# Two sets of level tiles and a keys-first order for the delta heads in an encoder layer kernel

## The chip, the cores and the metric

The kernel runs on one core of one Trainium2 chip. The metric is the device time of one execution in microseconds (us); the time before is the median of three runs, 1550.36 us (1548.67 to 1551.51).

## What is computed

One layer of a bidirectional encoder over 1024 tokens of width 1024: a mixer, a cross-attention into 256 memory tokens, and a SwiGLU layer, each with a norm before and after. Only the mixer is touched. It projects the normed input once; some columns feed a windowed attention with rotary positions, others a gated DeltaNet that runs over the sequence in both directions.

```python
h = _rms_norm(x, g_mix_pre[l])
proj = h @ w_in[l]
aq, ak, av, dqkv, dgate, dalpha, dbeta = jnp.split(proj, IN_SPLITS, axis=-1)
aq = _rope(aq.reshape(b, s, ATTN_HEADS, ATTN_HEAD_DIM), positions)
...
attn_o = _window_attention(aq, ak, av, attn_sink[l])
dn_o = _gated_deltanet(dqkv, dgate, dalpha, dbeta, ...)
mix = jnp.concatenate([attn_o, dn_o], axis=-1) @ w_out[l]
```

Within a chunk the DeltaNet solves a unit lower triangular system. For head, direction and chunk, `k` the normed keys:

```python
decay = jnp.exp(jnp.where(incl, g[..., :, None] - g[..., None, :], -jnp.inf))
kb = k * beta[..., None]
lower = jnp.where(strict, jnp.einsum('bhnid,bhnjd->bhnij', kb, k) * decay, 0.0)
tmat = lower + jnp.eye(c, dtype=jnp.float32)
sol = lax.linalg.triangular_solve(tmat, rhs, left_side=True, lower=True, unit_diagonal=True)
```

The kernel uses chunks of 128 tokens (8 of them), which gives the same result. There are 4 delta heads and 2 directions.

## The kernel before

**Stages.** The normed input is turned into `hT` (high and low parts of each 512-token half). A projection of 128 columns (`proj`, `gemm_b`, L261) is 48 matrix products into two `pg` banks, of which there are three; the weights are loaded (`load_w`) and split into `whi` and `wlo`. Then come, in this order:

1. *Delta stage* (to about 227 us): for each of the heads 0 to 3, keys, queries and values are projected (`delta_proj`), convolved over 5 taps on ScalarE and VectorE (`conv`), and prepared (`prep`). `prep` makes the decay matrix `E`, turns keys, values and queries with TensorE (`turned`), takes lengths, forms `U` (keys by keys, times `E`, stored to `d_u`), the scaled keys and values in one tile `kv` (stored to `d_kv`), and the masked query products `pm` (stored to `d_pz`). `base_inverse(g)` follows for each pair of heads: it reads the 32x32 diagonal blocks of `U` back into a tile `V`, builds `A`, and solves all 32x32 triangles at once with 60 small VectorE operations (L534, L536), then stores the results to `d_inv`. Each of its tiles has one buffer. `ORDER_1` is the order of these steps; `save` holds the last `pm` stores back until the second inverse's loads are issued.
2. *Levels and projections* (227 to about 360 us). `levels(h)` joins the 32x32 inverses to 64 and then to 128: 20 small loads (`fetch`, L551) put the blocks on the diagonals of the wide tiles `D5`, `D6`, `Z0`, `Z1` (128 x 8 x 128) and into `m5`, two loads bring `Ul`, and then TensorE, ScalarE and VectorE take turns: transposes of `Ul` (L576) give `L5` and `L6`, a product and its copy `bs` and a second product (L585, L591) give `z5`, which is put into `D6` and `Z`, and the same once more with `L6`, `mov6` gives the outer blocks of `Z`, which are stored. There is one set of the wide tiles, so each head's fetches wait for the head before. `ORDER_2` mixes the levels with the attention projections `A0` to `A4` (`A4` makes the keys), the values `V`, the gates `G0` to `G3` and pairs of windows `W`. `attn_proj` multiplies a projected half by sine and cosine (`sn`, `rop`), sends `sn` through four transfers that rotate its partitions into `rot2`, adds, splits into `qhi` and `qlo`, and stores both. `value_proj` copies a half to `vT` and transposes it (`ptv`, L749).
3. *Windows, scan, memory keys* (to about 594 us), under `ORDER_3`. A window loads its queries `qs`, takes scores `psw` against the keys `khi`, `klo`, does a softmax on VectorE and ScalarE, transposes (`ptw`) and multiplies with the values (`pow`). The scan (`psc`) reads `d_kv` and `d_pz`.
4. The rest of the layer, which starts with the mixer's output projection (L1016).

**What sets the order.** The three `ORDER` lists say in which order the steps are written. A scheduler then fixes each engine's own order when the program is built; on the chip each engine runs its list strictly in order. All transfers are issued by SyncE's queue, one after the other; a transfer that waits holds all that stand behind it. A tile's tag and `bufs` give the number of buffers that its users share: the next user of a buffer waits until the last one has been read.

Of the kernel before, what the change touches and what calls it, by code (L numbers as in the profile page):

```python
# [19 lines left out]
P = 128  # L20
# [55 lines left out]
def tile_hybrid_block(  # L76
# [121 lines left out]
    def small():  # L198
        return ps.tile([P, 512], F32, tag="ps", name="ps")
# [76 lines left out]
    def conv(pp, ci):  # L276
        cp = tcv.tile([P, S + 4], F32, tag="cp", name="cp", bufs=2)
        nc.gpsimd.memset(cp[:, 0:2], 0.0)
        nc.gpsimd.memset(cp[:, S + 2:S + 4], 0.0)
        acc = tcv.tile([P, S], F32, tag="acc", name="acc", bufs=3)  # L280
        taps = [cols[:, t * 12 + ci:t * 12 + ci + 1] for t in range(5)]
        for hf in range(2):
            nc.scalar.copy(cp[:, 2 + hf * HALF:2 + (hf + 1) * HALF], pp[hf])
            nc.scalar.activation(acc[:, hf * HALF:(hf + 1) * HALF], pp[hf], AF.Identity, scale=taps[2])  # L284
        for t in (0, 1, 3, 4):
            nc.vector.scalar_tensor_tensor(acc, cp[:, t:t + S], taps[t], acc, ALU.mult, ALU.add)  # L286
        nc.scalar.activation(acc, acc, AF.Silu)
        return acc
# [125 lines left out]

    unsaved = []

    def save(after=None):

        while unsaved:
            with ExitStack() as order_:  # L420
                if after:
                    order_.enter_context(tc.issue_after(after.ins))
                nc.sync.dma_start(*unsaved.pop(0))

    def prep(h, kc, qc, vc):

        g, hh = h // 2, h % 2
        for src, slot in ((kc, 2), (qc, 3)):
            nc.sync.dma_start(d_kv[g][:, :, hh, slot].rearrange("c p n -> p c n"), src.rearrange("p (c n) -> p c n", c=NT))

        def part(b):
            c4 = slice(4 * b, 4 * b + 4)

            def turned(src):
                p_ = small()
                for j in range(4):
                    o = (4 * b + j) * P
                    nc.tensor.transpose(p_[:, j * P:(j + 1) * P], src[:, o:o + P], ident)
                return p_.rearrange("p (c n) -> p c n", c=4)

            def lengths(pk):
                sq = t2.tile([P, 4, P], F32, tag="jk", name="jk")
                nc.scalar.activation(sq, pk, AF.Square)
                ss = t2.tile([P, 4], F32, tag="ss4", name="ss4", bufs=4)
                nc.vector.tensor_reduce(ss, sq, axis=AX.X, op=ALU.add)
                return ss

            pa = small()
            n = 0
            for d, (mi, ml) in enumerate((("mUi", mL_r), ("mLi", mU_r))):  # L450
                for part in (ghi, glo):
                    gm = t2.tile([P, 4, P], F32R, tag="gm", name="gm")
                    if d:
                        for j in range(4):
                            nc.scalar.mul(gm[:, j], cm[mi], part[:, d, h, 4 * b + j:4 * b + j + 1])
                    else:
                        nc.vector.tensor_tensor(gm, bc(part[:, d, h, c4], 2, (P, 4, P)), bc(cm[mi], 1, (P, 4, P)), ALU.mult)
                    nc.tensor.matmul(pa, ml, gm.rearrange("p c n -> p (c n)"), start=(n == 0), stop=(n == 3))
                    n += 1
            E = t2.tile([P, 4, P], F32, tag="E", name="E")  # L460
            nc.scalar.activation(E, pa.rearrange("p (c n) -> p c n", c=4), AF.Exp)

            yield
            kv = t2.tile([P, 4, 2, P], F32, tag="kv", name="kv")
            pk = turned(kc)
            ss = lengths(pk)
            nc.scalar.copy(kv[:, :, 0, :], pk)
            sl = t2.tile([P, 2, 4], F32, tag="rs4", name="rs4", bufs=4)
            nc.vector.tensor_scalar(sl[:, 0], ss, EPS, None, ALU.add)
            nc.gpsimd.tensor_tensor(sl[:, 1], sl[:, 0], phalf[:, :4], ALU.pow)  # L470
            nc.vector.reciprocal(sl[:, 0], sl[:, 0])
            nc.vector.tensor_tensor(beta2[:, g, :, hh, c4], beta[:, :, h, c4], bc(sl[:, 0], 1, (P, 2, 4)), ALU.mult)
            yield
            p_ = small().rearrange("p (c n) -> p c n", c=4)
            for j in range(4):
                kk = kc[:, (4 * b + j) * P:(4 * b + j + 1) * P]
                nc.tensor.matmul(p_[:, j, :], kk, kk, start=True, stop=True)
            U = t2.tile([P, 4, P], F32, tag="U", name="U")
            nc.vector.tensor_tensor(U, p_, E, ALU.mult)
            nc.sync.dma_start(d_u[g][hh, c4].rearrange("c p n -> p c n"), U)  # L480
            yield
            nc.vector.tensor_tensor(kv[:, :, 1, :], turned(vc), bc(sl[:, 1], 2, (P, 4, P)), ALU.mult)
            nc.sync.dma_start(d_kv[g][c4, :, hh, 0:2].rearrange("c p s n -> p c s n"), kv)
            yield
            ss = lengths(turned(qc))
            nc.vector.tensor_scalar(epsq[:, h, c4], ss, EPS * P, EPS * EPS * P, ALU.mult, ALU.add)
            yield
            p_ = small().rearrange("p (c n) -> p c n", c=4)
            for j in range(4):
                o = slice((4 * b + j) * P, (4 * b + j + 1) * P)  # L490
                nc.tensor.matmul(p_[:, j, :], kc[:, o], qc[:, o], start=True, stop=True)
            pc = t2.tile([P, 4, P], F32, tag="pc", name="pc")
            nc.vector.tensor_tensor(pc, p_, E, ALU.mult)
            for d, mi in enumerate(("mUi", "mLi")):
                pm = t2.tile([P, 4, P], F32, tag="pm", name="pm", bufs=3)
                nc.vector.tensor_tensor(pm, pc, bc(cm[mi], 1, (P, 4, P)), ALU.mult)
                unsaved.append((d_pz[g][d][c4, :, hh, 0].rearrange("c p n -> p c n"), pm))
            if h < 3:
                save()

        together([part(b) for b in range(2)])

    def base_inverse(g):
# [42 lines left out]
    def levels(h):  # L546
# [128 lines left out]
    def window_keys(g):  # L675
        keys[g] = tw.tile([P, S], F32R, tag="khi", name="khi"), tw.tile([P, S], F32R, tag="klo", name="klo", bufs=1)
        for kk, src in zip(keys[g], d_k):
            for r in range(2):
                nc.sync.dma_start(f32(kk[64 * r:64 * r + 64]), src[64 * g:64 * g + 64, :])
# [14 lines left out]
    wins, wins_done = [], [0]  # L694
    kqv = {0: kqv0}

    def delta_proj(h):
        kqv[h] = kqv.get(h, [])
        for i in (1, 0, 2)[len(kqv[h]):]:
            kqv[h].append(conv(proj(dcols(i, h)), 4 * i + h))  # L700

# [4 lines left out]

    issue(ORDER_1, {"D": delta_proj, "P": lambda h: prep(h, *kqv[h]), "B": base_inverse})
    pp_.close()
# [5 lines left out]
    tw.tile([P, 384], F32, tag="sc", name="sc", bufs=8)  # L714
    vhl = tw.tile([P, NT + 1, 2, 2, 64], F32R, tag="vhl", name="vhl", bufs=1)[:, 0:NT]
    tl_ = p1.enter_context(pool("tl", 2))
    wide_sets = [[tl_.tile([P, NT, P], F32, tag=f"{n}{i}", name=n, bufs=1) for n in ("D5", "D6", "Z0", "Z1")] for i in range(1)]
    for t in wide_sets[0]:
        nc.gpsimd.memset(t, 0.0)

    def attn_proj(ct):
        pp = proj(w_in[:, ct * P:(ct + 1) * P])
        dst = [t[ct * P:(ct + 1) * P, :] if ct < 4 else t for t in (d_q if ct < 4 else d_k)]
        for hf in range(2):
# [10 lines left out]
            nc.vector.tensor_tensor(rop, rop, rot, ALU.add)  # L735
            hl = [trp.tile([P, HALF], F32R, tag=t, name=t) for t in ("qhi", "qlo")]
            split(*hl, rop)
# [787 lines left out]
```

## Time and profile before

| | us |
|---|---|
| median of the three runs | 1550.36 |
| profiled execution | 1555.78 |
| its span in the trace | 1554.1 |
| TensorE busy | 1497.3 (96%) |
| VectorE busy | 1055.9 (68%) |
| ScalarE busy | 719.6 (46%) |
| end of the first base inverse (`V` written) | 228.6 |
| end of the second (`V` written) | 292.2 |
| first window product | 311.8 |
| last projection product of the stage | 359 |
| first scan product | 382.9 |

Times in the profile are counted from the span's start. PE is the matrix unit of TensorE, PEld its weight load, DVE VectorE, ACT ScalarE, POOL GpSimd, SP or SPq SyncE's queue. In a row of the timeline stand the start, the duration, the engine, the line, what is written and read, the number of instructions, and in brackets the idle time before it and what ended that. The granted clock is a share of the full TensorE clock.

### The profile page before, as it was taken

The page shows a single profiled execution, that of the slowest core. Times are in us where ns is not written, and L with a number is a line of the kernel's source. Part 1 is how long each engine was busy: PE and PEld are TensorE (multiplying, and loading weights), DVE is VectorE, ACT ScalarE, POOL GpSimd, SP SyncE. Part 2 cuts the span into 40 slices and gives each one's busy share as a digit, 9 for nine tenths or more (in the row PEclk, how much of TensorE's full clock was granted, in tenths as well). Part 3 has the DMA queues.
Part 4 walks back from the last instruction along what each step waited for, and adds up shares of the span by engine and source line. Part 5 has one row for each costly group of instructions (what it writes and reads, how often), then busy time and mean ns, then how long its engine had stood idle before and what let it go on. Part 6 is the DMA issues. An engine that isn't in the chain of part 4 may idle for free.

```text
span 1554.1 us, 20931 instructions
## 1 busy us (share of the span) xinstructions
PE 1497.3 (96%) x7451; PEld 1258.1 (81%) x7451; DVE 1055.9 (68%) x1750; ACT 719.6 (46%) x1380; POOL 308.3 (20%) x305
## 2 busy tenths in 40 slices
PE   6999999898899999999999999999999999999998
PEld 5888888787899877888888777888888888888786
DVE  6777898766898766443447367776867554687665
ACT  6666552246556755454335574332323332454532
POOL 2000110000003201163102221433533333000021
PEclk9999999997999999999999999999999999999999
DMA  6244456867987584354213264344434334863354
GB/s 211 69 136 128 125 157 160 217 179 245 319 278 247 164 283 165 119 190 148 82 55 123 85 200 141 111 135 129 134 122 132 102 102 141 288 193 102 108 175 165
DMA packets 267366, 247.16 MB, mean 159 GB/s; under 512 B 39016, under 2 KB 204797, under 8 KB 267261
## 3 DMA queue, kind: packets, MB, share of 16 engines
q1 hardware_dynamic: 267261, 245.82, 50.7%
q8 instruction: 59, 0.97, 0.3%
q14 instruction: 46, 0.38, 0.1%
HBM read 173.65 MB, written 69.50 MB: 156 GB/s over the span
## 4 chain that ended last, share of the span: by engine, by line
PE 80%; DVE 6%; DMA 6%; ACT 3%; issue 2%; SPq 2%; POOL 0%; DVEq 0%; POOLq 0%; ACTq 0%
PE pg L261 13%; PE pmg L1016 10%; PE pD L1196 8%; PE pE L1196 8%; PE pA L1196 6%; PE pcq L261 6%; PE pdX L1386 6%; PE pdA L1386 4%; PE pB L1196 4%; PE psc L785 2%; PE pdX L1479 2%; PE pdD L1386 2%; DMA wraw<-in_w_ckv_dram 2%; PE pcs L1102 1%; PE pco L1128 1%
## 5 line engine op out<-in xcount | busy, mean ns | idle before, releaser
L102 ACT CAST whi<-wraw 128x1024 fp32r<-128x1024 f32 x108 | 113.5, 1051 | 173.3 <-PE pg L261 36.0
L103 DVE TENSOR_TENSOR wlo<-wraw,whi 128x1024 fp32r<-128x1024 f32 x78 | 95.5, 1225 | 77.7 <-ACT whi L102 75.0
L261 PE MATMUL pg<-hhi,whi 128*128 128x512 f32 x352 | 140.8, 401 | 0.2 <-DVE rop L730 0.2
L261 PE MATMUL pg<-hhi,wlo 128*128 128x512 f32 x352 | 140.2, 399 | 0.0
L261 PE MATMUL pg<-hlo,whi 128*128 128x512 f32 x352 | 139.9, 398 | 0.0
L1016 PE MATMUL pmg<-whi,b 128*128 128x512 f32 x384 | 118.4, 394 | 0.4 <-ACT b L102 0.4
L1196 PE MATMUL pA<-s,whi 128*128 128x512 f32 x352 | 109.5, 392 | 1.4 <-ACT m L1213 1.4
L103 POOL TENSOR_TENSOR wlo<-wraw,whi 128x1024 fp32r<-128x1024 f32 x30 | 73.8, 2460 | 143.3 <-ACT whi L102 143.2
L1016 PEld LDWEIGHTS pmg<-whi,b 128*128 128x128 f32 x384 | 71.3, 188 | 15.2 <-ACT b L102 1.3
L261 PEld LDWEIGHTS pg<-hhi,whi 128*128 128x128 f32 x352 | 67.3, 192 | 14.0 <-DVE rop L730 0.7
L261 PEld LDWEIGHTS pg<-hlo,whi 128*128 128x128 f32 x352 | 67.2, 191 | 13.2
L261 PEld LDWEIGHTS pg<-hhi,wlo 128*128 128x128 f32 x352 | 67.2, 191 | 13.1
L1196 PEld LDWEIGHTS pA<-s,whi 128*128 128x128 f32 x352 | 65.3, 188 | 15.2 <-ACT m L1213 2.0
L1386 PE MATMUL pdX<-dhl,whi 128*128 128x512 f32 x264 | 76.1, 390 | 1.5 <-DVE zv L1441 0.8
L1016 PE MATMUL pmg<-wlo,b 128*128 128x512 f32 x192 | 71.5, 392 | 0.0
L1196 PE MATMUL pA<-s,wlo 128*128 128x512 f32 x176 | 68.7, 392 | 1.1 <-DVE wlo L103 1.1
L102 ACT CAST whi<-araw 128x1024 fp32r<-128x1024 f32 (+1 forms) x36 | 35.4, 984 | 69.9 <-PE pdX L1386 27.6
L1273 POOL TENSOR_TENSOR act<-act,up 128x512 f32<-128x512 f32 x33 | 50.1, 1519 | 89.1 <-DVE up L1272 53.1
L103 DVE TENSOR_TENSOR wlo<-araw,whi 128x1024 fp32r<-128x1024 f32 (+1 forms) x36 | 40.8, 1133 | 38.4 <-ACT whi L102 38.3
L286 DVE SCALAR_TENSOR_TENSOR acc<-cp,cols,acc 128x1024 f32<-128x1024 f32 x48 | 61.5, 1282 | 1.5 <-ACT acc L284 0.8
L1386 PEld LDWEIGHTS pdX<-dhl,whi 128*128 128x128 f32 x264 | 49.3, 188 | 12.8 <-issue 1.1
L1246 DVE TENSOR_TENSOR sr<-sr,wraw 128x512 f32<-128x512 f32 x22 | 37.8, 1716 | 29.8 <-POOL sr L1245 29.8
(409 smaller groups left out, 3976.7 us busy)
## 6 DMA issues: line engine op xcount, KB each, us to landing
wraw<-in_w_gate_up_dram SPq DMA_DIRECT2D x52, 512.0 KB, 4.0
kv<-d_kv SPq DMA_DIRECT2D x32, 512.0 KB, 6.6
wraw<-in_w_in_dram SPq DMA_DIRECT2D x22, 512.0 KB, 5.5
b<-in_w_down_dram SPq DMA_DIRECT2D x20, 512.0 KB, 6.8
araw<-d_as SPq DMA_DIRECT2D x20, 512.0 KB, 3.8
pz<-d_pz SPq DMA_DIRECT2D x32, 256.0 KB, 6.8
wraw<-in_w_ckv_dram SPq DMA_DIRECT2D x16, 512.0 KB, 6.4
wraw<-in_w_out_dram SPq DMA_DIRECT2D x16, 512.0 KB, 4.3
```

What stands on the lines that cost most here:

```text
L102: nc.scalar.copy(hi, src)
L103: (eng or nc.vector).tensor_tensor(lo, src, f32(hi), ALU.subtract)
L261: nc.tensor.matmul(p_, w[:, k, :], ah[a][:, k, :], start=(k == 0 and i == 0), stop=(k == nk - 1 and i == 2))
L286: nc.vector.scalar_tensor_tensor(acc, cp[:, t:t + S], taps[t], acc, ALU.mult, ALU.add)
L785: nc.tensor.matmul(out[:, d, h, :], lt[:, d, h, :], rt[:, d, h, :], start=True, stop=True)
L1016: nc.tensor.matmul(pp[t], act[a][:, k, tt], w_[:, kk, :], start=(k == 0 and i == 0), stop=(k == KT - 1 and i == 2))
L1102: nc.tensor.matmul(pp[:, t2_, :], q[a][:, ct, tt], kr_[b_][:, ct, :], start=(j == 0 and i == 0), stop=(j == 1 and i == 2))
L1196: nc.tensor.matmul(out_, w[a][:, k, :], xx[b_][:, k, :], start=(start and k == 0 and i == 0), stop=(k == HK - 1 and i == 2), skip_group_ch ...
L1246: nc.vector.tensor_tensor(s[1], s[0], a_[:, 0:HK], ALU.subtract)
L1273: nc.gpsimd.tensor_tensor(o_, o_, up, ALU.mult)
L1386: nc.tensor.matmul(banks[t], a[:, k - k0, tt], w, start=(first and k == 0 and i == 0), stop=(k == NB - 1 and i == 2), skip_group_check=not ...
L1479: nc.tensor.matmul(X[t], a[:, k], w[:, k0 + k], start=False, stop=(k0 + k == NB - 1 and i == 2), skip_group_check=True)
```

## The change

- `ORDER_1` is finer: `k` and `r` are the two halves of the old `prep` (`prep_keys`, `prep_rest`), and `Dih` projects one of keys (1), queries (0) or values (2) of one head. The keys of heads 0 and 1 are projected and prepared first, and those of heads 2 and 3 ahead of the second base inverse, which stands ahead of their queries and values.
- The tile `kv` becomes `kt` and `vt`, each stored by itself. `E`, `U`, `acc` and the small scales get more buffers; `pc` shares `U`'s.
- The wide tiles come in two sets, used by even and odd heads; `L5`, `L6` and `Ul` share five buffers instead of six.
- To make room, `qhi` and `qlo` take the buffers of `sn` and `rot2` (`vT` shares with them), `khi` has one buffer instead of two, and `vhl` loses a spare slice.
- `save` goes; the `pm` stores are issued where they are written.

```diff
-ORDER_1 = "D0 P0 D1 P1 D2 B0 P2 D3 P3 B1".split()
+LT = 5
+ORDER_1 = "k0 k1 D00 D20 r0 D01 D21 r1 D12 B0 D13 k2 k3 D02 B1 D22 r2 D03 D23 r3".split()
 ORDER_2 = "L0 L1 G0 G1 A4 V A0 A1 L2 L3 W W W A2 A3 G2 G3 W".split()
...
-        acc = tcv.tile([P, S], F32, tag="acc", name="acc", bufs=3)
+        acc = tcv.tile([P, S], F32, tag="acc", name="acc", bufs=5)
...
-    ws = [load_w(dcols(i, 0), KT, P, after=xload[t]) for i, t in ((1, 1), (0, 3))]
+    ws = [load_w(dcols(1, i), KT, P, after=xload[t]) for i, t in ((0, 1), (1, 3))]
...
-    kqv0 = [conv(pps[0], 4), conv(pps[1], 0)]
+    kqv = {(1, h): conv(pps[h], 4 + h) for h in range(2)}
...
-    def prep(h, kc, qc, vc):
+    def prep_keys(h, b):
...
+        E = decay[h, b] = t2.tile([P, 4, P], F32, tag="E", name="E", bufs=4)
+        nc.scalar.activation(E, pa.rearrange("p (c n) -> p c n", c=4), AF.Exp)
+        yield
+        kt = t2.tile([P, 4, P], F32, tag="kt", name="kt", bufs=3)
+        pk = turned(kc, b)
+        ss = lengths(pk)
+        nc.scalar.copy(kt, pk)
+        nc.sync.dma_start(d_kv[g][c4, :, hh, 0].rearrange("c p n -> p c n"), kt)
...
+        U = t2.tile([P, 4, P], F32, tag="U", name="U", bufs=3)
+        nc.vector.tensor_tensor(U, p_, E, ALU.mult)
+        nc.sync.dma_start(d_u[g][hh, c4].rearrange("c p n -> p c n"), U)
+        yield
+
+    def prep_rest(h, b):
...
+        ss = lengths(turned(qc, b))
+        nc.vector.tensor_scalar(epsq[:, h, c4], ss, EPS * P, EPS * EPS * P, ALU.mult, ALU.add)
+        yield
...
+        pc = t2.tile([P, 4, P], F32, tag="U", name="pc", bufs=3)
+        nc.vector.tensor_tensor(pc, p_, decay[h, b], ALU.mult)
+        for d, mi in enumerate(("mUi", "mLi")):
+            pm = t2.tile([P, 4, P], F32, tag="pm", name="pm", bufs=3)
+            nc.vector.tensor_tensor(pm, pc, bc(cm[mi], 1, (P, 4, P)), ALU.mult)
+            nc.sync.dma_start(d_pz[g][d][c4, :, hh, 0].rearrange("c p n -> p c n"), pm)
+        yield
+        vt = t2.tile([P, 4, P], F32, tag="kt", name="vt", bufs=3)
+        nc.vector.tensor_tensor(vt, turned(vc, b), bc(scales[h, b][:, 1], 2, (P, 4, P)), ALU.mult)
+        nc.sync.dma_start(d_kv[g][c4, :, hh, 1].rearrange("c p n -> p c n"), vt)
+        yield
...
-            load = nc.sync.dma_start(V[q:64:4], d_u[g].rearrange("h c p n -> (h c) p n")[:, r, r])
-        if g:
-            save(load)
+            nc.sync.dma_start(V[q:64:4], d_u[g].rearrange("h c p n -> (h c) p n")[:, r, r])
...
-        D5a, D6a, *Za = wide_sets[0]
+        D5a, D6a, *Za = wide_sets[h % 2]
...
-                return tl_.tile([P, 4, P], F32, tag=name, name=name, bufs=2)
+                return tl_.tile([P, 4, P], F32, tag="L", name=name, bufs=LT)
...
-        keys[g] = tw.tile([P, S], F32R, tag="khi", name="khi"), tw.tile([P, S], F32R, tag="klo", name="klo", bufs=1)
+        keys[g] = tw.tile([P, S], F32R, tag="khi", name="khi", bufs=1), tw.tile([P, S], F32R, tag="klo", name="klo", bufs=1)
...
-    wide_sets = [[tl_.tile([P, NT, P], F32, tag=f"{n}{i}", name=n, bufs=1) for n in ("D5", "D6", "Z0", "Z1")] for i in range(1)]
-    for t in wide_sets[0]:
+    wide_sets = [[tl_.tile([P, NT, P], F32, tag=f"{n}{i}", name=n, bufs=1) for n in ("D5", "D6", "Z0", "Z1")] for i in range(2)]
+    for t in wide_sets[0] + wide_sets[1]:
         nc.gpsimd.memset(t, 0.0)
...
-            hl = [trp.tile([P, HALF], F32R, tag=t, name=t) for t in ("qhi", "qlo")]
+            hl = [trp.tile([P, HALF], F32R, tag=t, name=n) for t, n in (("rot", "qhi"), ("rot2", "qlo"))]
```

The scheduler's orders that follow from it are shown in the prediction, at the places it speaks of.

More of the change, by code (lines that the diff above doesn't have):

```diff
@@ L413, in together @@
             gens = [g for g in gens if next(g, g) is not g]
[L415 to L423, printed above, removed]
-    def prep(h, kc, qc, vc):
-        g, hh = h // 2, h % 2
[L428 to L501, printed above, removed]
@@ new lines, in turned, with lengths @@
+    def turned(src, b):
+        p_ = small()
+        for j in range(4):
+            o = (4 * b + j) * P
+            nc.tensor.transpose(p_[:, j * P:(j + 1) * P], src[:, o:o + P], ident)
+        return p_.rearrange("p (c n) -> p c n", c=4)
+    def lengths(pk):
+        sq = t2.tile([P, 4, P], F32, tag="jk", name="jk")
+        nc.scalar.activation(sq, pk, AF.Square)
+        ss = t2.tile([P, 4], F32, tag="ss4", name="ss4", bufs=4)
+        nc.vector.tensor_reduce(ss, sq, axis=AX.X, op=ALU.add)
+        return ss
@@ new lines, in prep_rest @@
+    def prep_rest(h, b):
+        g, hh = h // 2, h % 2
+        c4 = slice(4 * b, 4 * b + 4)
+        qc, kc, vc = (kqv[i, h] for i in range(3))
+        if b == 0:
+            nc.sync.dma_start(d_kv[g][:, :, hh, 3].rearrange("c p n -> p c n"), qc.rearrange("p (c n) -> p c n", c=NT))
+        ss = lengths(turned(qc, b))
+        nc.vector.tensor_scalar(epsq[:, h, c4], ss, EPS * P, EPS * EPS * P, ALU.mult, ALU.add)
+        yield
+        p_ = small().rearrange("p (c n) -> p c n", c=4)
+        for j in range(4):
+            o = slice((4 * b + j) * P, (4 * b + j + 1) * P)
+            nc.tensor.matmul(p_[:, j, :], kc[:, o], qc[:, o], start=True, stop=True)
+        pc = t2.tile([P, 4, P], F32, tag="U", name="pc", bufs=3)
[8 more added lines that the diff above has]
+        nc.sync.dma_start(d_kv[g][c4, :, hh, 1].rearrange("c p n -> p c n"), vt)
+        yield
@@ L694, in tile_hybrid_block, with delta_proj @@
     wins, wins_done = [], [0]
[L695 to L700, printed above, removed]
+    def delta_proj(i, h):
+        kqv[i, h] = conv(proj(dcols(i, h)), 4 * i + h)
     def issue(order, table):
@@ L705, in issue @@
             table[o[0]](*(int(c) for c in o[1:]))
-    issue(ORDER_1, {"D": delta_proj, "P": lambda h: prep(h, *kqv[h]), "B": base_inverse})
+    issue(ORDER_1, {"D": delta_proj, "k": lambda h: together([prep_keys(h, b) for b in range(2)]),
+                    "r": lambda h: together([prep_rest(h, b) for b in range(2)]), "B": base_inverse})
     pp_.close()
```

28 lines of the change are left out of this document (27 added, 1 removed).

## The prediction

> **What bounds the kernel now.** First the busy line of the page, then the table of windows, cut at the places where the stages change.
>
> ```profile
> PE 1497.3 (96%) x7451; PEld 1258.1 (81%) x7451; DVE 1055.9 (68%) x1750; ACT 719.6 (46%) x1380; POOL 308.3 (20%) x305
> ```
>
> ```profile
> 0.00:227.00 227.00, 212.08 (x1066) 177.70 (x1067) 179.16 (x298) 138.51 (x248) 24.19 (x62) 1.00 0.46 135
> 227.00:360.00 133.00, 125.81 (x671) 107.62 (x669) 97.91 (x217) 43.85 (x103) 3.40 (x5) 0.95 0.75 196
> 360.00:410.00 50.00, 42.20 (x234) 36.52 (x234) 35.18 (x94) 30.54 (x74) 2.55 (x7) 0.76 0.82 270
> 410.00:594.00 184.00, 174.42 (x1180) 157.45 (x1178) 147.75 (x357) 118.11 (x289) 25.68 (x36) 0.98 0.79 248
> ```
>
> The columns are the stretch, its length, the busy time of PE, PEld, DVE, ACT and POOL, the granted TensorE clock, the DMA share and GB/s. TensorE is the bound nearly everywhere, so time is lost only where it idles or is granted less clock; I count idle + (1 - clock) x busy. From 227 to 360 (levels, attention and gate projections, first windows) that is 7.2 + 0.05 x 125.8 = 13.5 us; from 360 to 410 (windows alone, then the scan's start) 7.8 + 0.24 x 42.2 = 17.9 us. Together **31.4 us**, which the change can refill or add to. Behind 410 nothing that it touches is late, and the code there is the same. Up to 227 there is next to nothing to win: the table of waits for 100 to 227 us has one row.
>
> ```profile
> PE ps L438 <- DVE kv L482: 1.7, 1, 1.7
> ```
>
> In slices of 10 us and by waits, the 31.4 us lie here:
>
> ```profile
> 250.00:260.00 10.00, 7.97 (x46) 7.18 (x46) 8.10 (x21) 4.03 (x12) 0.00 (x0) 0.83 0.63 172
> 360.00:370.00 10.00, 9.27 (x53) 8.36 (x53) 5.84 (x19) 5.52 (x15) 0.00 (x0) 0.79 0.29 81
> 370.00:380.00 10.00, 6.80 (x23) 4.73 (x23) 5.34 (x15) 7.89 (x18) 1.01 (x4) 0.50 0.78 229
> 380.00:390.00 10.00, 9.77 (x62) 8.77 (x61) 8.62 (x22) 6.35 (x16) 1.34 (x3) 0.86 1.02 402
> 390.00:400.00 10.00, 7.22 (x49) 5.74 (x47) 7.54 (x22) 4.51 (x12) 0.20 (x1) 0.99 1.01 292
> 400.00:410.00 10.00, 9.13 (x53) 8.92 (x54) 7.84 (x19) 6.27 (x15) 0.00 (x0) 0.67 0.98 345
> ```
>
> ```profile
> PE psw L633 <- DMA qs<-d_q: 3.9, 1, 3.9
> PE ptv L749 <- ACT vT L746: 2.0, 1, 2.0
> PE pck L916 <- ACT whi L102: 2.0, 1, 2.0
> ```
>
> The worst slice, 370 to 380, is one where the projections have run out and the windows hang on their own softmax.
>
> **The change, part by part.** *Delta stage.* The keys-first order leaves the matrix work as it is. The `kv` store is split in two halves, `kt` and `vt`, so 8 stores become 16, and six of the eight scaled values stand ahead of the first inverse on VectorE where all eight stood:
>
> ```profile
> L482 DVE TENSOR_TENSOR kv<-ps,rs x8: 660/686/692, 89.7 to 214.5; 128x512 f32<-128x512 f32 x8
> ```
>
> (count; shortest, median and longest in ns.) Two of them are 1.4 us, and TensorE's own work covers them: it waited 1.7 us there in all. I take 0, bounds -2 and +3 (the one wait gone, or one like it twice over). B1 still writes the tiles `V`, `A` and `bB` of B0, one buffer each, so the second inverse starts only after B0's stores; it can win only what stands in front of it.
>
> *Head 0's levels.* Here lies the first term. Rotary products of `A4`'s two halves (`sn`, `rop`), rotated copies `rot2` and split results `qhi`, `qlo` now share two buffers of two tags. The second half's `sn` gets the buffer of the first half's, which is free only when its four rotating DMAs have landed. SyncE before (numbers are buffers; 2552/2551 first half, 2568/2567 second):
>
> ```order
> L551 DMA Z1_2123<-d_inv01_112 32x8x32
> L572 DMA Ul_2272<-d_u0_109 128x4x128
> L572 DMA Ul_2276<-d_u0_109 128x4x128
> L734 DMA rot2_2552<-sn_2551 32x512 x4
> L734 DMA rot2_2568<-sn_2567 32x512 x2
> ```
>
> SyncE in the change (2576/2575 first half, 2592/2591 second; 2140 to 2143 are the second set):
>
> ```order
> L547 DMA D6_2141<-d_inv00_111 32x8x32
> L547 DMA Z0_2142<-d_inv01_112 32x8x32
> L547 DMA m5_2273<-d_inv01_112 32x8x32 x4
> L547 DMA Z1_2143<-d_inv01_112 32x8x32
> L568 DMA Ul_2296<-d_u0_109 128x4x128
> L568 DMA Ul_2300<-d_u0_109 128x4x128
> L727 DMA rot2_2576<-sn_2575 32x512 x2
> ```
>
> Two of the first half's rotations go out ahead of the fetches, further up; the other two now stand behind 44 transfers, 20 fetches and 2 `Ul` for each of heads 0 and 1, where they stood behind 20 fetches and what lies between. VectorE, which frees the projection's PSUM, now has the second half's products behind the sum that needs those two:
>
> ```order
> L728 TENSOR_TENSOR rop_2574<-rop_2574,rot2_2576 128x512
> L530 TENSOR_TENSOR tmpb_1717<-A_1713 128x240
> L722 TENSOR_TENSOR sn_2591<-pg_2525,sinT_590 128x512
> L723 TENSOR_TENSOR rop_2590<-pg_2525,cosT_591 128x512
> ```
>
> And TensorE has nothing to put between head 0's level products any more; the next projection, `pg_2686`, needs the bank that `rop_2590` reads:
>
> ```order
> L262 MATMUL pg_2613<-hhi1_232,wlo_2609 128x512
> L572 MATMUL ps_2181<-ident_68,Ul_2175 128x128 x4
> L572 MATMUL ps_2188<-ident_68,Ul_2179 128x128 x4
> L581 MATMUL ps_2195<-m5_2152,L5_2173 128x32 x4
> L581 MATMUL ps_2202<-m5_2152,L5_2177 128x32 x4
> L587 MATMUL ps_2209<-bs_2200,D5_2136 128x32 x4
> L587 MATMUL ps_2225<-bs_2207,D5_2136 128x32 x4
> L581 MATMUL ps_2241<-mov6_2220,L6_2174 128x64 x4
> L581 MATMUL ps_2248<-mov6_2236,L6_2178 128x64 x4
> L587 MATMUL ps_2255<-bs_2246,D6_2137 128x64 x4
> L587 MATMUL ps_2264<-bs_2253,D6_2137 128x64 x4
> L262 MATMUL pg_2686<-hhi0_146,whi_2682 128x512
> ```
>
> Before, 18 products of the next projection came first and the rest lay between. The times are from the timeline of before, rows of SyncE, VectorE, TensorE and ScalarE:
>
> ```profile
> 238.57 0.75 SPq L551 DMA_DIRECT2D m<-d_inv  x1
> 249.09 0.94 SPq L551 DMA_DIRECT2D Z<-d_inv  x2
> 250.12 0.95 SPq L572 DMA_DIRECT2D Ul<-d_u  x2
> 251.12 3.75 SPq L734 DMA_DIRECT2D rot<-sn  x6
> ...
> 235.42 0.68 DVE L730 TENSOR_TENSOR rop<-pg,cosT 128x512 f32<-128x512 f32 x1
> 255.18 0.69 DVE L735 TENSOR_TENSOR rop<-rop,rot 128x512 f32<-128x512 f32 x1 [1.45 <-DMA rot<-sn]
> 262.87 0.69 DVE L729 TENSOR_TENSOR sn<-pg,sinT 128x512 f32<-128x512 f32 x1
> 263.47 0.68 DVE L730 TENSOR_TENSOR rop<-pg,cosT 128x512 f32<-128x512 f32 x1
> 271.39 0.43 DVE L608 TENSOR_SCALAR Z<-ps 64x256 f32<-64x256 f32 x1
> ...
> 245.27 0.39 PE L261 MATMUL pg<-hhi,wlo 128*128 128x512 f32 x1
> 249.58 1.91 PE L585 MATMUL ps<-m,L 128*128 128x32 f32 x16
> 251.32 0.48 PE L261 MATMUL pg<-hhi,whi 128*128 128x512 f32 x1
> ...
> 255.64 0.27 ACT L587 COPY bs<-ps 128x128 f32<-128x128 f32 x1
> ```
>
> Twenty fetches and one `d_pz` store went out from 238.57 to 250.12, 0.55 us each; a rotation takes 3.75 / 6 = 0.63. So in the change: 238.6 + 2 x 0.63 + 44 x 0.55 = 264.0 for the two late rotations, 265.3 when both are issued; the fourth of the six of before was issued at about 253.6 and its sum ran at 255.18, so 1.6 us to land: 266.9. One `tmpb` step and two products (start to start 0.6) later the bank is free, about **268**. Projection products come (249.58 - 245.27) / 19 = 0.227 apart, and the value projection's last one ends near 245.5 (before, the next projection's first 18 stand ahead of 249.58). TensorE is thus held for 22.5 us. What it does inside is head 0's own work: four rounds of 16 records at (251.32 - 249.58) / 16 = 0.109, 7.0, and 0.8 for transposes (estimate from the same pace). Lost: 22.5 - 7.8 = 14.7, say **15 us**. The levels alone would hold it nearly as long: `Ul` goes out at 238.6 + 1.3 + 12.1 = 252, and from the second `bs` at 255.64 to the `Z` at 271.39 the old chain, with products in between, took 15.7. Bounds: 8 (fetches start 2 us sooner with the first inverse, and half the chain's queueing falls away) and 20 (the rotations are served after the second set's writes too).
>
> Behind so long a hole the clock must come back. Before, it was low after the 2.03 us wait for `vT`:
>
> ```profile
> 259.51 0.63 PE L261 MATMUL pg<-hlo,whi 128*128 128x512 f32 x1
> 262.92 0.59 PE L261 MATMUL pg<-hhi,whi 128*128 128x512 f32 x1
> 263.34 0.40 PE L261 MATMUL pg<-hlo,whi 128*128 128x512 f32 x1
> ```
>
> The last two are 0.42 apart against 0.227; some 7 us of low clock from 256 to 263 cost 3, and I charge **3** here. The Trainium skill, "TensorE: Matmul & The Clock Gate", Part 1, has the clock halved after an idle window of about 3.4 us and restored after one busy window; by that the 2.03 us wait of before ought to have cost nothing, and the trace disagrees (0.83 granted). By the page the charge would be half of that window, an estimate of 1.7, and the forecast a good microsecond lower.
>
> *Value copies.* `vT` takes `rot` buffers that only now come free, behind the second half's rotations and `d_k` stores: the 2.0 us wait moves, and I take **2** (0 to 4). *Heads 1 and 2* no longer wait for head 0's tiles, but head 2's tiles do wait for head 0's stores: **2** (0 to 4), a guess of the size of the `vT` wait. *First windows.* Their keys and queries now stand on SyncE behind all fetches of heads 2 and 3. Before:
>
> ```profile
> 303.09 1.12 SPq L679 DMA_DIRECT2D khi<-d_k  x2
> 305.53 2.60 SPq L625 DMA_DIRECT2D qs<-d_q  x4
> 311.75 0.55 PE L633 MATMUL psw<-khi,qs 128*128 128x256 f32 x1 [3.87 <-DMA qs<-d_q]
> 290.17 2.02 DVE L538 TENSOR_TENSOR V<-A,bB 128x1024 f32<-128x1024 f32 x1
> ```
>
> After the second inverse's stores (about 290) come 42 fetches and `Ul` at 0.55, 8 rotations at 0.63 and a dozen stores at some 0.45: `khi` at about 324, first product near 332. TensorE gets there with 192 projection products (43.5 us at 0.227), two heads' levels (2 x 7.8) and 7 us of the losses above: 268 + 66 = 334. So the 3.9 us wait shrinks to **2** (0 to 6). Head 3's levels and the first windows then stand together with few projection products between; **3** (0 to 6).
>
> *What is given back.* Head 3's level products end ahead of 64 projection products in the new order; before they came behind the last of them:
>
> ```order
> L262 MATMUL pg_3706<-hhi1_232,whi_3701 128x512
> L587 MATMUL ps_3080<-bs_3071,D6_2141 128x64 x4
> L262 MATMUL pg_3706<-hlo1_233,whi_3701 128x512
> L587 MATMUL ps_3089<-bs_3078,D6_2141 128x64 x4
> L660 MATMUL pow_3184<-ph_3190,vhl_2132 128x512
> ```
>
> So the hole from 360 to 380 can close: its two rows are worth 3.9 + 0.21 x 9.3 + 0.5 x 6.8 = 9.3. Of the remaining 8.6 to 410 (the wait for `whi` and the scan's start) little is touched; I leave **8** of the 17.9 standing (0 to 16).
>
> Sum: 15 + 3 + 2 + 2 + 2 + 3 + 8 = 35 against 31.4: **+3.6 us**. The profiled execution (1555.78) becomes 1559.4; the runs' median is 5.4 lower, so **1554.0 us**, slower by 0.23%. A measurement of this kernel tells about 0.2%, 3.1 us, from no change.
>
> **Rivals.** *The second hole closes (faster).* With head 3 done 64 products ahead of the end, the windows and the scan's first step run into each other, and from where the projections end to the scan's second step 1 us is lost and not 8; the two waits that follow the fetches come at 1 each: 15 + 3 + 2 + 1 + 1 + 2 + 1 = 25, -6.4, 1544. It decides once less than 4.4 of the 17.9 is left there. For it: the largest loss of before lies just where the second set works. Against: the windows' chain is softmax on ACT and DVE (7.9 and 5.3 of 10 in the worst slice), which no level tile shortens. *Fetch pile-up (much slower).* SyncE is the queue: if the late rotations and then the windows' loads come at their upper bounds, 20 + 3 + 4 + 3 + 6 + 4 + 9 = 49, +18, 1568. It decides once `khi` goes out after about 330, some 4 us behind TensorE. For it: a row of 20 fetches already took 11.5 us of SyncE. Against: TensorE gets there late as well. *A swap (no change).* The second inverse is no earlier since it shares the first one's tiles, and the hole only moves from 370 to 250: 31 for 31, 1550.
>
> **How the numbers follow.** Forecast 0.43, of which 0.07 lies within 0.2% since its sum is so near to it; pile-up 0.14; second hole closed 0.33; swap 0.10. Slower 0.50, same 0.17, faster 0.33. The range 1541 to 1568 reaches over both outer cases and leaves out their far ends; the forecast's own is 1550 to 1560.
>
> **What would show it.** In the waits of the changed kernel: a TensorE idle time of some 10 us or more in all between 245 and 270, with `pg` released by DVE `rop` or `ps` by level tiles; the first 8 projection products behind it 0.43 apart; `khi` issued at 320 or later; the slice from 370 to 380 at full clock. The forecast is wrong if TensorE passes 250 to 265 without a gap, or if the windows' hole stands as before.

## The result, and the profile after

The changed kernel takes **1568.01 us** (median of four, 1566.60 to 1569.60) against 1550.93 beside it: a ratio of 1.0112, 95% interval 1.0097 to 1.0127. Slower was forecast, but by 3.6 us; it is 17, and the time lies at the very edge of the stated range, just outside. One execution of an experiment below (of `e6_share_split`) took 3839 us and is left out of its ratio.

The same table of windows as before, for the changed kernel (stretch, length, busy PE, PEld, DVE, ACT, POOL, granted clock, DMA share, GB/s):

```profile
0.00:227.00 227.00, 213.52 (x1072) 178.92 (x1073) 183.78 (x300) 140.86 (x250) 27.89 (x66) 1.00 0.48 139
227.00:360.00 133.00, 118.82 (x596) 102.53 (x595) 86.00 (x199) 36.77 (x93) 3.73 (x4) 0.86 0.66 168
360.00:410.00 50.00, 45.30 (x268) 37.83 (x267) 34.95 (x86) 33.65 (x71) 3.41 (x7) 1.00 0.79 258
410.00:635.00 225.00, 208.72 (x1337) 185.61 (x1336) 171.44 (x398) 135.11 (x323) 37.59 (x49) 0.98 0.75 237
```

And the last stretch of the kernel before, which the prediction left out:

```profile
410.00:635.00 225.00, 215.33 (x1358) 190.86 (x1357) 169.51 (x380) 134.29 (x315) 37.75 (x52) 0.98 0.73 231
```

With the prediction's measure, idle + (1 - clock) x busy, the stretches lose: up to 227, 13.5 (before 14.9); 227 to 360, 14.2 + 16.6 = 30.8 (before 13.5); 360 to 410, 4.7 (before 17.9); 410 to 635, 16.3 + 4.2 = 20.5 (before 9.7 + 4.3 = 14.0). So the hole behind 360 did close, 17 us were lost ahead of it, and 6.5 us behind it, where the prediction saw nothing.

The stretch from 240 to 410 in slices of 10 us, of the changed kernel:

```profile
240.00:250.00 10.00, 5.25 (x23) 3.82 (x21) 1.89 (x5) 1.04 (x1) 0.00 (x0) 0.82 0.55 110
250.00:260.00 10.00, 8.72 (x40) 8.28 (x39) 8.60 (x22) 2.67 (x9) 0.00 (x0) 0.50 0.47 93
260.00:270.00 10.00, 9.16 (x36) 8.33 (x36) 8.79 (x22) 2.44 (x6) 0.00 (x0) 0.50 1.00 273
...
330.00:340.00 10.00, 4.36 (x24) 3.72 (x22) 3.35 (x8) 1.64 (x3) 0.00 (x0) 0.83 1.14 266
340.00:350.00 10.00, 8.92 (x39) 8.29 (x40) 8.83 (x23) 6.49 (x19) 1.11 (x1) 0.60 0.87 256
...
370.00:380.00 10.00, 10.00 (x50) 8.36 (x49) 4.80 (x14) 6.75 (x15) 1.61 (x4) 1.00 0.41 140
```

Two holes, around 243 to 267 and 331 to 350; from 370 to 380, the worst slice before, TensorE is full. The longest waits of TensorE from 227 to 640 us, by what ended them (total, times, longest):

```profile
PE pow L660 <- ACT ph L103: 6.8, 5, 4.1
PE pmg L1009 <- DVE z L1013: 5.2, 1, 5.2
PE ps L572 <- DMA Ul<-d_u: 4.7, 1, 4.7
PE psw L629 <- DMA qs<-d_q: 4.6, 2, 4.3
```

The timeline of the changed kernel, rows of SyncE, VectorE and TensorE (start, duration, idle time before in brackets):

```profile
233.96 0.53 SPq L547 DMA_DIRECT2D m<-d_inv  x1
257.04 1.00 SPq L568 DMA_DIRECT2D Ul<-d_u  x2
258.09 1.15 SPq L727 DMA_DIRECT2D rot<-sn  x2
326.46 1.17 SPq L675 DMA_DIRECT2D khi<-d_k  x2
...
261.80 0.69 DVE L728 TENSOR_TENSOR rop<-rop,rot 128x512 f32<-128x512 f32 x1
262.73 0.68 DVE L722 TENSOR_TENSOR sn<-pg,sinT 128x512 f32<-128x512 f32 x1
263.33 0.68 DVE L723 TENSOR_TENSOR rop<-pg,cosT 128x512 f32<-128x512 f32 x1
...
242.90 0.39 PE L262 MATMUL pg<-hhi,wlo 128*128 128x512 f32 x1
248.01 1.09 PE L572 MATMUL ps<-ident,Ul 128*128 128x128 f32 x4 [4.73 <-DMA Ul<-d_u]
266.62 0.78 PE L262 MATMUL pg<-hhi,whi 128*128 128x512 f32 x1
335.11 0.58 PE L629 MATMUL psw<-khi,qs 128*128 128x256 f32 x1 [4.31 <-DMA qs<-d_q]
```

The first hole lies where it was forecast: the last projection product starts at 242.90 (forecast: ends near 245.5), the next at 266.62 (forecast 268); the late rotations leave after both heads' fetches, the sum runs at 261.80 and only then the second half's `sn` and `rop`, which frees the bank at 264.0. Head 0's bare chain of levels ends last, 2.6 us later. So on the chip it is this chain that holds TensorE: it begins with a wait of 4.73 us for `Ul` and then runs at a granted clock of 0.50. That no projection product stands between its links is the built order, in which the next one waits for the late bank.

### The profile page after: what moved, and what is told of

It reads as the page before. It is cut to its first block, busy times and chain, and to the rows that moved or that the text cites. A ratio compares the mean times of both kernels' runs of the same rounds, so it can differ in the third digit from the quotient of the medians.

```text
span 1565.7 us, 20959 instructions
## 1 busy us (share of the span) xinstructions
PE 1499.0 (96%) x7451; PEld 1259.2 (80%) x7451; DVE 1060.3 (68%) x1750; ACT 722.6 (46%) x1382; POOL 317.1 (20%) x309
## 5 line engine op out<-in xcount | busy, mean ns | idle before, releaser
L262 PEld LDWEIGHTS pg<-hhi,whi 128*128 128x128 f32 x352 | 67.1, 191 | 13.5 <-ACT hhi L103 0.3
L262 PEld LDWEIGHTS pg<-hlo,whi 128*128 128x128 f32 x352 | 66.9, 190 | 13.2
```

Source lines behind the costliest of these rows:

```text
L262: nc.tensor.matmul(p_, w[:, k, :], ah[a][:, k, :], start=(k == 0 and i == 0), stop=(k == nk - 1 and i == 2))
```

## The experiments

Each was run in three rounds beside the kernel before, whose median moved between 1549.7 and 1551.2 over the calls. The ratios are to its runs; they are taken from the single runs and can differ by 0.001 from the quotient of the medians. A builder's scheduler lays out all engines' orders anew at every edit, so each of these edits moves more than its own lines; what that does is told behind the last of them.

**First four: take the change apart.** `e1_share` is the kernel before with this:

```diff
-            hl = [trp.tile([P, HALF], F32R, tag=t, name=t) for t in ("qhi", "qlo")]
+            hl = [trp.tile([P, HALF], F32R, tag=t, name=n) for t, n in (("rot", "qhi"), ("rot2", "qlo"))]
```

> The kernel before, with one edit of the change: qhi and qlo take the buffers of sn and rot2. Theory 1 (the shared buffers make the hole between 243 and 267 us): a hole of some 15 us appears there and the time is about 1561 (+8 to +14 against 1551). Theory 2 (the second set of level tiles makes it, with 44 transfers ahead of the late rotations): about 1551 to 1555. Theory 3 (the keys-first order of the delta stage costs the time): 1551, no change.

Measured 1570.32, ratio 1.0118 (1.0098 to 1.0137). `e2_levels` is the kernel before with all of the change's edits behind the delta stage.

> The kernel before, with the whole level part of the change (two sets, five shared L buffers, one khi buffer, shared qhi and qlo) and the old delta stage. Theory 1 and theory 2: 1563 to 1570, nearly all of the 17 us. Theory 3: 1551 to 1555. If it comes out under 1551, the keys-first order is what spoils a level part that is good by itself.

Measured 1570.26, 1.0122 (1.0096 to 1.0148). `e3_delta` is the change with this taken back, and the L, khi and vhl tiles with it:

```diff
-        D5a, D6a, *Za = wide_sets[h % 2]
+        D5a, D6a, *Za = wide_sets[0]
```

> The change, with one set of level tiles and the old L, khi and vhl buffers; the keys-first order and the shared qhi and qlo stay (they do not fit apart). Theory 1: like e1, 1558 to 1566. Theory 2: 1551 to 1555. Theory 3: 1565 to 1570.

Measured 1571.54, 1.0126 (1.0105 to 1.0147). `e4_a4first`:

```diff
-ORDER_2 = "L0 L1 G0 G1 A4 V A0 A1 L2 L3 W W W A2 A3 G2 G3 W".split()
+ORDER_2 = "A4 V L0 L1 G0 G1 A0 A1 L2 L3 W W W A2 A3 G2 G3 W".split()
```

> The change, with A4 and V written ahead of L0 and L1 in ORDER_2, so that the rotations of A4 stand ahead of the fetches on SyncE. If the first hole comes from rotations behind fetches (theory 1 with 2), the gap between 243 and 267 is gone and the time falls by 12 us or more, to 1556 or less. If head 0's bare chain of levels holds TensorE by itself, the gap stays at 8 us or more and the time is 1562 or more. If the 5 us wait at the mixer's output projection has its own cause, that wait stays at 4 to 6 us in either case.

Measured 1559.24, 1.0049 (1.0032 to 1.0066).

The edit that made room is as slow alone as the whole change: one line, no second set, no new order of the heads, 19 us. All three kernels that contain it lie within 1.5 us of each other and within 4 us of the change. Theory 1 holds in kind and was too small in size (8 to 14 forecast; e3 lies above its range too). The other two are not needed for this loss, which does not say that the second set and the new order are free (see e9 and e10).

In e4, which has the rotations ahead of the fetches, 9 of the 17 us go; it missed the 1556 expected. Its windows (227 to 360, 410 to 635) tell where:

```profile
227.00:360.00 133.00, 118.20 (x600) 102.47 (x599) 85.72 (x198) 37.53 (x94) 7.71 (x10) 0.86 0.66 172
410.00:635.00 225.00, 216.26 (x1381) 190.30 (x1381) 177.21 (x403) 138.03 (x328) 39.52 (x53) 1.00 0.77 244
```

Ahead of 360 it still loses 14.8 + 16.5 = 31.3, as the change does. The first hole is smaller (9.7 us lost from 240 to 270, for 16.8 in the change), but the `qs` wait has grown to 7.7 us, and 320 to 350 now loses 18.1 for 11.0. What goes lies behind 410, 8.7 for 20.5, the 5.2 us wait at the mixer's output projection among it. Part of the hole moved, and it was not shown why the time behind 410 came back.

In e1 the rows of VectorE and the windows show the hole of the change, without a second set in the kernel:

```profile
233.05 0.68 DVE L729 TENSOR_TENSOR sn<-pg,sinT 128x512 f32<-128x512 f32 x1
233.64 0.68 DVE L730 TENSOR_TENSOR rop<-pg,cosT 128x512 f32<-128x512 f32 x1
264.95 0.69 DVE L735 TENSOR_TENSOR rop<-rop,rot 128x512 f32<-128x512 f32 x1
265.87 0.68 DVE L729 TENSOR_TENSOR sn<-pg,sinT 128x512 f32<-128x512 f32 x1
...
227.00:360.00 133.00, 113.96 (x579) 98.67 (x577) 82.38 (x179) 28.99 (x71) 2.62 (x3) 0.87 0.66 169
410.00:635.00 225.00, 213.84 (x1389) 190.76 (x1387) 174.74 (x408) 139.32 (x335) 38.65 (x47) 0.98 0.76 245
```

Between the first half's `sn` at 233.05 and the second half's at 265.87 lie 33 us; in the kernel before they ran at 232.18 and 234.81. With the prediction's measure e1 loses 19.0 + 14.8 = 33.9 from 227 to 360 and 11.2 + 4.3 = 15.4 behind 410: as slow as the change in all, but with nearly all of its loss ahead of 360.

**A buffer or an order?** Three buffers for each shared tag against a loop written otherwise. `e5_share3` is e1 with `bufs=3` on every tile of the two tags.

> The kernel of e1, with three buffers for each of the two shared tags in place of two. Theory A (the second half's products wait for a free buffer, held by the rotations): the hole between 246 and 268 shrinks and the time falls to 1556 or less. Theory B (what counts is the order in which the users of a tag are written: the second half's sn is written behind the first half's qhi, and so is put behind the first half's sum on VectorE, whatever is free): the time stays at 1566 to 1572.

Measured 1569.58, 1.0117 (1.0093 to 1.0140): nothing. VectorE of e5:

```profile
232.89 0.68 DVE L729 TENSOR_TENSOR sn<-pg,sinT 128x512 f32<-128x512 f32 x1
265.17 0.68 DVE L735 TENSOR_TENSOR rop<-rop,rot 128x512 f32<-128x512 f32 x1
266.09 0.68 DVE L729 TENSOR_TENSOR sn<-pg,sinT 128x512 f32<-128x512 f32 x1
```

A free third buffer was there from the start, and `sn` still stood behind the sum. So it is not the buffer that holds it but the order in which the users of one tag are written: `sn` of half 1 is written behind `qhi` of half 0, which needs the sum. To test this, the loop was written in two, in `e6_share_split` on e1, in `e7_after_split` on the change and in `e8_a4_split` on e4:

```diff
         for hf in range(2):
...
             for q in range(4):
                 o = 32 * (q ^ 1)
                 nc.sync.dma_start(rot[32 * q:32 * q + 32], sn[o:o + 32])
+            halves.append((sl, rop, rot))
+        for sl, rop, rot in halves:
             nc.vector.tensor_tensor(rop, rop, rot, ALU.add)
```

> The kernel of e1 with two buffers for each shared tag, but attn_proj written with the products and rotations of both halves first, and the sums and splits of both behind them. Theory B: the second half's sn and rop are back in front, the bank of PSUM is free early, and most of the 19 us go: 1553 to 1560. Theory A: both halves now need all buffers at once, no gain: 1566 to 1572.

Measured 1564.17, 1.0087 (1.0070 to 1.0104), between the two ranges. The second half's `sn` is back in front:

```profile
235.56 0.69 DVE L730 TENSOR_TENSOR sn<-pg,sinT 128x512 f32<-128x512 f32 x1 [1.44 <-PE pg L261]
```

That confirms the order. But only 6 of the 19 us go: from 240 to 290 e6 still loses 11.6 us (e1 22.1, the kernel before 5.1), now with a wait of 6.3 us for a `Z` of VectorE in head 0's levels.

> The change, with attn_proj written as in e6. Theory B: the first hole falls from some 14 us of lost time to a few, and the time to 1553 to 1559; the wait for qs near 331 stays, since the fetches of heads 2 and 3 still stand ahead of it. Theory A: 1565 to 1570.

Measured 1554.77, 1.0029 (1.0017 to 1.0041).

> The change, with A4 and V ahead of L0 and L1 (e4) and attn_proj as in e6. If the two repair one and the same hole: 1553 to 1559, about the lower of e4 and e7. If they repair different ones: under 1551, faster than before. If e4's gain came from the rotations alone and nothing else is left: no better than e4, 1557 to 1560.

Measured 1554.45, 1.0028 (1.0019 to 1.0038).

Same tiles, same buffers, same two sets: the loop's form takes 13.2 us from the change. VectorE and the two windows of e7:

```profile
234.30 0.69 DVE L723 TENSOR_TENSOR sn<-pg,sinT 128x512 f32<-128x512 f32 x1
237.28 0.69 DVE L724 TENSOR_TENSOR rop<-pg,cosT 128x512 f32<-128x512 f32 x1 [2.29 <-issue]
258.01 0.69 DVE L730 TENSOR_TENSOR rop<-rop,rot 128x512 f32<-128x512 f32 x1 [4.31 <-DMA rot<-sn]
...
227.00:360.00 133.00, 119.16 (x618) 102.97 (x618) 89.78 (x205) 39.46 (x96) 1.83 (x4) 0.90 0.68 175
410.00:635.00 225.00, 216.83 (x1356) 190.29 (x1356) 174.22 (x393) 136.96 (x327) 40.99 (x53) 0.99 0.76 238
```

The second half's products now run 20 us ahead of the first sum. The time is the one expected, the reason only in part: from 240 to 270 e7 still loses 12.5 us for 16.8, where a few were expected. VectorE now stands 4.3 us before the first sum, and TensorE waits 5.1 us for a `mov` of VectorE. Of the lost time, 5 us go between 227 and 360 (13.8 + 11.9 = 25.8 for 30.8), and 10 behind 410 (8.2 + 2.2 = 10.3 for 20.5), while 360 to 410 takes 2.4 more. Most of the gain thus comes late, outside the hole that was aimed at, and how it follows from the order of `sn` was not shown. The gains of e4 and e7 do not add up: together (e8) they are no better than e7. They do not lie in the same place either: e8 gains 9 ahead of 360 and 4 behind 410.

**Without the sharing.** The whole of two sets does not fit beside own buffers for `qhi` and `qlo`; these four come as near as memory allows. `e9_keys_first`: one set, three `acc` buffers. `e10_z_sets`: the old delta stage, a second pair of `Z0`, `Z1` only. `e11_both_z`: both. `e12_both_d6z`: the change with this, and four `acc` buffers:

```diff
-            hl = [trp.tile([P, HALF], F32R, tag=t, name=n) for t, n in (("rot", "qhi"), ("rot2", "qlo"))]
+            hl = [trp.tile([P, HALF], F32R, tag=t, name=t, bufs=1) for t in ("qhi", "qlo")]
...
-    wide_sets = [[tl_.tile([P, NT, P], F32, tag=f"{n}{i}", name=n, bufs=1) for n in ("D5", "D6", "Z0", "Z1")] for i in range(2)]
+    wide_sets = [[tl_.tile([P, NT, P], F32, tag=f"{n}{i}", name=n, bufs=1) for n in ("D5", "D6", "Z0", "Z1")[1 * i:]] for i in range(2)]
+    wide_sets[1] = wide_sets[0][:1] + wide_sets[1]
```

> The keys-first order alone: the change with one set of level tiles, the old L, khi and vhl buffers, qhi and qlo in tags of their own, and three acc buffers as before (five do not fit). If the shared tags carry the whole loss, about 1550, at most 1553. If the keys-first order costs something by itself, 1554 to 1560. If it gains, since the second inverse comes sooner: 1544 to 1548.

> The second set alone, as far as it fits without the sharing: the kernel before with a second pair of Z0 and Z1 (D5 and D6 stay single), five shared L buffers, one khi buffer, qhi and qlo in tags of their own. If the second set fills the hole of 360 to 380 us as the second rival had it: 1543 to 1548. If the loads that it lets out early only stand before others: 1551 to 1558.

> Keys-first order and second Z pair together, qhi and qlo in tags of their own, three acc buffers. If the shared tags are the whole cause of the loss, this is at or under 1551; if sets and order lose by themselves, it lies at 1554 to 1562, near the kernel with the split loop (1554.8).

> The change with qhi and qlo in tags of their own of one buffer each, a second set of D6, Z0 and Z1 (D5 single) and four acc buffers. Same theories as for e11: at or under 1551 if the shared tags are all, 1554 to 1562 if not. With one buffer each, a second half's split waits for the first half's store, which may cost up to 3.

Measured 1560.91 (1.0066, 1.0045 to 1.0086), 1570.67 (1.0133, 1.0113 to 1.0153), 1556.62 (1.0039, 1.0027 to 1.0051) and 1554.30 (1.0023, 1.0007 to 1.0039). With tags of their own and nearly two sets (e12) the kernel is where the split loop has it, and the first hole is gone: 2.0 us are lost from 240 to 270. So the sharing is shown from both sides: e1 puts the hole in, e12 takes it away. Each half of the change alone is worse than both and lies above the ranges given for it (e9 by 1 us, e10 by 13): e9 pays in the delta stage,

```profile
0.00:227.00 227.00, 204.79 (x1012) 170.22 (x1013) 183.97 (x297) 131.37 (x241) 25.66 (x60) 0.98 0.47 133
```

8.7 us less matrix work done by 227 than in the change. That its three `acc` buffers are the reason is likely and not shown: e11, with three, has 206.0 there, e12, with four, 211.1, the change, with five, 213.5. And e10 has a wait for `mov6` in head 0's levels, which the kernel before has not:

```profile
280.16 3.65 PE L586 MATMUL ps<-mov,L 128*128 128x64 f32 x16 [6.39 <-DVE mov L604]
```

The parts do not add up, and the second set has not been shown to gain by itself.

**What is left.** `e13_share3_split` is e6 with three buffers, `e14_own_split` is e12 with the split loop, `e15_split_w` and `e16_own_w` are e7 and e12 with

```diff
-ORDER_2 = "L0 L1 G0 G1 A4 V A0 A1 L2 L3 W W W A2 A3 G2 G3 W".split()
+ORDER_2 = "L0 L1 G0 G1 A4 V A0 A1 W L2 L3 W W A2 A3 G2 G3 W".split()
```

`e17_before_split` is the kernel before with the split loop alone, `e18_own_a4` is e12 with `A4 V` first.

> The kernel of e1 with both repairs: three buffers for each shared tag and the products of both halves written first. If the 19 us of e1 are made of an order (6 us, repaired by e6 alone) and of buffers that are held (nothing by themselves in e5, since the order hid them), the two together bring it back to 1549 to 1554. If something else in the sharing costs, it stays at 1560 or more.

> The kernel of e12 (qhi and qlo in tags of their own) with the products of both halves written first. With tags of their own the order is free already: the same as e12 within 3 us, 1551 to 1557. If the order still matters there: 1545 to 1550.

> The kernel of e7 (the change with the split loop) with the first pair of windows written ahead of L2 and L3 in ORDER_2. If the wait for qs behind the fetches of heads 2 and 3 (5.2 us and the low clock after it) is what is left of the loss, that wait goes and the time falls to 1547 to 1551. If it is hidden anyway or moves to the second pair of windows: 1552 to 1557.

> The kernel of e12 with the first pair of windows ahead of L2 and L3. With the first hole gone and the windows' loads in front, the second rival's closing of the 360 to 380 hole can show itself: 1543 to 1549. If the windows only take projection products away from the levels of heads 2 and 3: 1552 to 1560.

> The kernel before with the split loop alone, nothing shared: a control for e6 and e13. If the split loop costs by itself in this kernel (its order has head 0's levels closer together: 62 projection products and then 8 and 8 with 6 between), 1557 to 1563, and the sharing with three buffers is then repaired in full by e13. If the split loop is neutral there, 1549 to 1553, and the shared tags keep some 10 us of cost that neither buffers nor order explain.

> The kernel of e12 (tags of their own) with A4 and V ahead of L0 and L1. If putting the rotations first helps beyond the repair of the first hole: 1545 to 1550, a version faster than both. If it did nothing but repair that hole: 1551 to 1557, as e12.

Measured 1561.49 (1.0069, 1.0053 to 1.0085), 1551.24 (1.0003, 0.9991 to 1.0015), 1560.06 (1.0057, 1.0040 to 1.0073), 1559.27 (1.0055, 1.0038 to 1.0072), 1559.52 (1.0054, 1.0033 to 1.0075) and 1559.25 (1.0058, 1.0041 to 1.0076).

e17 is the control that mattered: in the kernel before, where nothing is shared, the split loop alone costs 8.5 us. Against it e13, with sharing, costs 2.0 more, which the two intervals do not tell from nothing. In time, then, sharing with a free buffer and the order set right is nearly free, and most of what stayed in e13 may be the split loop's own. The traces agree in the total and not in place: e13 loses 10.7 from 240 to 270 and 4.4 from 360 to 410, e17 2.6 and 18.6. That also bounds what any of these differences can tell: an edit that frees one thing moves the whole layout, by 5 to 8 us in e15 to e18 (against e7, e12, the kernel before and e12), and each time to the worse. e15 and e16 brought the first window forward (309.6 us for 332.1 in e7, 299.4 for 310.3 in e12) and lost time all the same, so the late `qs` is not what remains. e15 and e18 lie above both ranges given for them. e14 is level with the kernel before. No version was faster than it.

## Why the prediction was wrong

*The first hole: right in place and size, half right in its cause.* Forecast 245.5 to 268, 15 us lost and 3 of clock. Measured 242.9 to 266.6; the three slices lose 5.7 + 5.6 + 5.4 = 16.8 against 18 (idle and clock from their rows). The shares are not those forecast: 6.9 us are idle and 9.9 low clock, most of that inside the hole. Behind it the first eight projection products stood some 0.43 apart, as the prediction's sign had it, from 266.6 to 270.2; that cost 1.7 us and not 3. The idle time was less than the 10 us named as a sign, about 5 from 245 to 270, and the one long wait ended with `Ul`, not with `rop` or a level tile. The late rotations, the products behind the sum and the bare chain of levels were all there, the last two ending 2.6 us apart. What was wrong in its reading: the late second half was put down to a buffer held by the rotations and to 44 transfers, half of them let out by the second set. e5 showed that a free buffer changes nothing, and e1 that one set is enough; it is the order of a shared tag's users.

*Value copies and heads 1 and 2: too dear.* 4 us set, under 1 lost between 270 and 330. *First windows and head 3: too cheap.* `khi` left at 326.5 (forecast 324) and the first product ran at 335.1 (forecast 332), but TensorE was there by 331 and not 334; with the low clock behind it (0.60 from 340 to 350) 330 to 350 alone cost 11, against 5 set. *The hole behind 360: closed further than forecast,* 4.7 against 8. These errors cancel: the sum was 35 and the two stretches lost 30.8 + 4.7 = 35.5. That they agree is luck. *The delta stage,* set at 0, lost 1.4 us less than before.

*The steps that failed.* "Behind 410 nothing that it touches is late, and the code there is the same": the lines are the same, the order is not, and 6.5 us were lost there. The second half of the mixed outputs is read back behind the last window's store. SyncE of the changed kernel, TensorE where it waits, and SyncE of the kernel before:

```profile
588.57 0.58 SPq L665 DMA_DIRECT2D d_mix<-ao  x1
589.21 5.65 SPq L1051 DMA_DIRECT2D b<-d_mix  x4
...
605.29 1.22 PE L1009 MATMUL pmg<-whi,s 128*128 128x512 f32 x2 [5.20 <-DVE z L1013]
```

```profile
573.75 0.59 SPq L669 DMA_DIRECT2D d_mix<-ao  x1
575.45 5.02 SPq L1058 DMA_DIRECT2D b<-d_mix  x4
```

The last window's output is stored 14.8 us later; `b` follows 13.8 later, its casts and splits stand on ScalarE and VectorE ahead of the evictions `z`, and TensorE waits 5.2 us for a bank. That the late first windows alone caused this does not hold: e7 and e4 read `b` later still (594.1 and 594.3) and have no such wait. What differs is the order on ScalarE, here in the change and then in e7:

```profile
595.29 1.05 ACT L103 CAST b<-b 128x1024 fp32r<-128x1024 f32 x1 [4.48 <-DMA b<-d_mix]
603.03 0.60 ACT L1012 ACTIVATE z<-pmg 128x512 f32<-128x512 f32 x1
...
592.77 0.60 ACT L1014 ACTIVATE z<-pmg 128x512 f32<-128x512 f32 x1
598.11 1.05 ACT L103 CAST b<-b 128x1024 fp32r<-128x1024 f32 x1 [1.17 <-DMA b<-d_mix]
```

In the change the casts of the late `b` stand ahead of the `z` that would free the bank; in e7 the first four `z`, and in e4 the first three, stand ahead of the casts. In the kernel before the casts stand first as well, but `b` comes so early (the first cast at 584.5, the first `z` at 591.6) that TensorE does not wait for a `z` there. No run changed this order by itself.

The second failing step is the offset: "the runs' median is 5.4 lower" was carried over to the changed kernel. The profiled execution of before was one of its slowest (1555.78; nearly all others lie between 1546 and 1554), that of the change is near its median (1567.54 for 1568.01). The traces are 11.6 us apart, the medians 17.1. Of the 14 us of error the tail is 6.5 and the offset 5.4; the other 2 are not placed.

*The rivals.* "The second hole closes" happened, and did not win. "Fetch pile-up" has the right time, 1568, but its mechanism was only there in part: `khi` went out at 326, short of its 330, and e1 is as slow with `khi` out at 316.9. "A swap" came nearest to what the stretch from 227 to 410 did, a hole moved, 35.5 for 31.4.

## What to carry to other kernels

Giving two kinds of tiles one tag to save memory also ties the order of their users: before doing so, look whether any user is written behind one that depends on something slow; writing all early users first cost no memory here and took back 13 of 17 us. The same edit cost 8.5 us in the kernel before, where nothing was shared, so it is to be measured and not taken over. A sum over stalls must reach to where the two orders are alike again, not to where the edited lines end. And a difference against one profiled execution carries that execution's own deviation: look first where it lies among its runs.

## What the runs showed of the hardware

In the changed kernel TensorE waited 4.73 us for `Ul`. The first products behind the wait, at 248.01, already ran at half pace (1.09 us for four transposes, against 0.60 for four at 275.20 in the kernel before), and the granted clock stayed low: 0.50 in both slices from 250 to 270, although TensorE was shown busy for 8.72 and 9.16 of 10 us. Up to 266.6 this was short products of head 0's levels with gaps of up to 0.84 us; then projection products ran without gaps, the first eight some 0.43 apart, and from 270.5 they were 0.23 apart again. The prediction had charged the clock behind the hole; most of it was paid inside. In this chain, then, products that filled 9 of 10 us did not bring the clock back. Whether their shortness or the gaps between them kept it low, no run here separates.
